# Weight sums of a split-precision mLSTM layer: one sum moved into an accumulating DMA, the heads' work cut into small pieces, four operand buffers

## The chip, the cores and the metric

One core of a Trainium2 chip runs the whole kernel. The metric is the device time of one execution in microseconds (us), taken as the median of several executions; lower is better. Instructions go to TensorE (PE: matmuls, with PEld for its weight loads), VectorE (DVE), ScalarE (ACT), GpSimd (POOL) and SyncE (SP). Here SP does nothing but start DMAs, and POOL, after a few constants, nothing else either.

## The reference

One pre-norm residual layer with an mLSTM token mixer; 256 tokens, model width 4096, 8 heads, query and key width 256, value width 512, all in float32:

```python
hn = rms_norm(x, norm_w)
u = hn @ w_in                                   # 4096 x (4096 qk, 4096 v, 4096 og, 4096 z, 16 gates)
qk = silu(causal_dwconv(qk, conv_w, conv_b))    # 4 taps
# per head, in chunks of 128 tokens with carried state:
#   a = exp(decay) * (q k^T);  num = a v;  hc = num / max(|sum a|, exp(-m))
hn = hc * rsqrt(mean(hc * hc) + EPS) * out_norm_w
y = hn * sigmoid(og) * silu(z)
out = x + y @ w_out                             # 4096 x 4096
```

Nearly all of the arithmetic is the two products with the weight matrices.

## The kernel before

**Products in split precision.** A float32 operand is used as a sum of two parts of a narrower type, `hi` (a rounded copy, made by ACT, L134) and `lo` (the rest, a subtraction on DVE, L135). `matmul3` (L137) issues three matmuls for each product: hi x hi (L139), hi x lo (L140), lo x hi (L141). The activations (`lhs`) are split once; the weights stream through once, in blocks of 128 x 1024 (512 KB), and each block or sum of blocks that is used costs one ACT and one DVE instruction over 1024 columns (`operand`, L143).

**Pairs.** The weights are used in 19 passes, called pairs: two column groups of 512 at a time. For each head there is a pair `oz` (gates of the output), for heads 1 to 7 a pair `qkv`, and at the end four pairs `o0` to `o3` of the output projection. Head 0's query, key and value come from a first stage before them. A pair walks through the 4096 rows in 8 chunks of 512.

**Two kinds of chunk.** Even chunks (`FAST`) use a scheme with seven block products P1 to P7 (in place of eight) on four blocks 11, 12, 21, 22 of weights. It needs four sums of weight blocks, each a DVE addition of 1024 columns: 11+12 (L246, for P5), 22+11 (L252, for P6), 12+22 (L255, for P7), 21+22 (L258, for P4), all updated in place. So a fast chunk has 7 operands, 4 sums and 42 matmuls. Odd (plain) chunks have 4 operands and 48 matmuls. One fast and the plain chunk beside it are called a couple below: 11 operands, 4 sums, 90 matmuls, 8 loads. A pair is four couples.

**Buffers.** Loaded blocks lie in 7 buffers (tag `wraw`, L155); `hi` and `lo` have 3 buffers each (`wpool`, L67). A load starts on SP when the last reader of its buffer is done; ACT can make a `hi` when PE has finished the operand that had the buffer before.

**Combination.** After a pair its seven PSUM banks are put together by four ACT copies (L321) and seven DVE operations (L322 to L328), all written at once behind the pair's last matmul. Then follows the work of the head: convolution (`conv_qk`), decay, scores, values, gates (`gate_y`, L600) and the transposition of the result (`turn`), held in a list `stages` of which one is run at fixed shares (eighths) of the next pair. A head's result is spilled to memory from POOL's queue (L502) and read back in the last `oz` pair (`build_y`), where the left operands of the output projection are built.

**What sets the order.** Each engine runs its own list in order. A scheduler lays these lists out when the program is built, from the order of the code and its own estimates; the lists are fixed then.

Of the kernel before, what the change touches and what calls it, by code (L numbers as in the profile page):

```python
# [61 lines left out]
def mlstm_layer(ctx: ExitStack, tc: tile.TileContext, x, xT, norm_w, w_first, w_in, conv_w, conv_b, gate_b,  # L62
# [125 lines left out]
    lhs = {}  # L188

    def build(c, src):  # L190

        if c in FAST:
            flat = lhs_pool.tile([P, 2 * 7 * HK * P], F32R, name=f"lhs_{c}", tag=f"lhs{c}")
            L = flat.rearrange("p (two s j t) -> p two s j t", two=2, s=7, j=HK)
            a11, a12, a21, a22 = (src[:, j * HK:(j + 1) * HK, t * P:(t + 1) * P]
                                  for t, j in ((0, 0), (0, 1), (1, 0), (1, 1)))
# [9 lines left out]
            names = ("P1", "P2", "P4", "P5", "P6", "P3", "P7")  # L206
            lhs[c] = {s: [[L[:, part, i, j, :] for part in range(2)] for j in range(HK)]
                      for i, s in enumerate(names)}
        else:
            flat = lhs_pool.tile([P, 2 * 3 * CK * P], F32R, name=f"lhs_{c}", tag=f"lhs{c}")  # L210
            L = flat.rearrange("p (two s j t) -> p two s j t", two=2, s=3, j=CK)
            F = big(f"F_{c}", [P, CK, P])
# [5 lines left out]

    def build_x(c):
        src = big(f"xn_{c}", [P, CK, T])  # L220
        nc.sync.dma_start(src, xT[:, c * CK:(c + 1) * CK, :])
        for j in range(CK):
            k = c * CK + j
            nc.vector.scalar_tensor_tensor(src[:, j, :], src[:, j, :], nw[:, k:k + 1], rstdB,
                                           op0=OP.mult, op1=OP.mult)
# [444 lines left out]
```

## Time and profile before

| | us |
|---|---|
| median of 3 runs | 1843.99 (1841.7 to 1845.84) |
| the profiled execution | 1845.81 |
| its span, first to last instruction | 1844.1 |
| PE busy | 1773.2 (96%) |
| DVE busy | 1654.5 (90%) |
| ACT busy | 1135.5 (62%) |
| POOL busy | 12.1 (1%) |
| data moved by DMA | 365.67 MB, mean 198 GB/s |

Busy time is the union of an engine's instructions. Matmuls are pipelined: one is shown with some 390 ns, but in an undisturbed stretch the next one starts 0.23 us after it. So the time from one pair to the next, and the distance between matmul starts, tell more of PE's stalls than its busy share does. "Landing" of a DMA is counted from the issuing instruction's start.

### The profile page before, as it was taken

What the parts mean: (1) busy time and instruction counts of PE and PEld (TensorE: products, weight loads), DVE (VectorE), ACT (ScalarE), POOL (GpSimd) and SP (SyncE); (2) the same over time, 40 slices, a digit from 0 to 9 for tenths busy, and PEclk for the clock granted to TensorE, in tenths of its full rate; (3) what the DMA queues carried; (4) which work ended last, traced back from release to release, by engine and by line L of the source; (5) the groups of instructions that cost most, each with busy time, mean ns of one, the idle gap of its engine ahead of it and who ended that gap; (6) DMA issues with size and microseconds to landing.
All of it is one profiled execution on the core that took longest, in us unless ns stands there. A gap on an engine that the chain in (4) does not pass through costs nothing.

```text
span 1844.1 us, 21723 instructions
## 1 busy us (share of the span) xinstructions
PE 1773.2 (96%) x7804; PEld 1410.7 (77%) x7804; DVE 1654.5 (90%) x1882; ACT 1135.5 (62%) x1303; POOL 12.1 (1%) x29
## 2 busy tenths in 40 slices
PE   9888999999999999999999999999998899999998
PEld 8766787777777878787878787878776668787776
DVE  5799999998999899989998989898989998989887
ACT  6565765665566556656666666566656665565654
POOL 0000000000000000000000000000000000000000
PEclk9899999999999999999999999999999999999999
DMA  9654465556555555565556555655556556766563
GB/s 365 230 189 171 161 220 188 196 174 216 193 183 180 197 192 184 189 200 188 184 198 209 185 187 197 205 183 183 194 194 214 177 189 217 236 210 233 189 206 126
DMA packets 107724, 365.67 MB, mean 198 GB/s; under 512 B 12128, under 2 KB 12512, under 8 KB 107616
## 3 DMA queue, kind: packets, MB, share of 16 engines
q1 hardware_dynamic: 105360, 356.95, 57.9%
q0 software_dynamic: 1968, 6.82, 1.0%
q8 instruction: 61, 1.00, 0.2%
q10 hardware_dynamic: 288, 0.52, 0.1%
q14 instruction: 47, 0.39, 0.1%
HBM read 356.38 MB, written 7.86 MB: 198 GB/s over the span
## 4 chain that ended last, share of the span: by engine, by line
PE 69%; DVE 19%; issue 7%; ACT 3%; DMA 2%; SPq 0%; DVEq 0%; ACTq 0%
PE P_qkv L140 9%; PE P_qkv L141 9%; PE P_qkv L139 9%; PE P_oz L140 9%; PE P_oz L141 8%; PE P_oz L139 8%; PE P_o L140 4%; PE P_o L141 4%; PE P_o L139 4%; DVE wl_oz_P L135 2%; DVE wl_oz L135 2%; DVE lhs L135 1%; DVE w_oz L246 1%; DVE wl_o_P L135 1%; DVE wl_o L135 1%
## 5 line engine op out<-in xcount | busy, mean ns | idle before, releaser
L134 ACT ACTIVATE wh_oz_P<-w_oz 128x1024 fp32r<-128x1024 f32 x224 | 237.6, 1061 | 109.0 <-PE P_oz L141 91.7
L135 DVE TENSOR_TENSOR wl_oz_P<-w_oz,wh_oz_P 128x1024 fp32r<-128x1024 f32 x224 | 270.8, 1220 | 20.2 <-ACT wh_oz_P L134 18.4
L135 DVE TENSOR_TENSOR wl_qkv_P<-w_qkv,wh_qkv_P 128x1024 fp32r<-128x1024 f32 x196 | 237.1, 1221 | 43.4 <-ACT wh_qkv_P L134 40.7
L134 ACT ACTIVATE wh_qkv_P<-w_qkv 128x1024 fp32r<-128x1024 f32 x196 | 208.1, 1062 | 82.5 <-PE P_qkv L141 73.2
L140 PE MATMUL P_oz<-wl_oz,lhs 128*128 128x512 f32 x512 | 205.1, 401 | 11.4 <-DVE wl_oz L135 10.3
L134 ACT ACTIVATE wh_oz<-w_oz 128x1024 fp32r<-128x1024 f32 x128 | 135.5, 1059 | 128.0 <-PE P_oz L141 74.0
L139 PE MATMUL P_oz<-wh_oz,lhs 128*128 128x512 f32 x512 | 190.7, 401 | 18.4 <-ACT wh_oz L134 17.4
L134 ACT ACTIVATE wh_qkv<-w_qkv 128x1024 fp32r<-128x1024 f32 x112 | 118.8, 1061 | 143.1 <-PE P_qkv L141 126.4
L141 PE MATMUL P_oz<-wh_oz,lhs 128*128 128x512 f32 x512 | 201.6, 394 | 0.0
L140 PE MATMUL P_qkv<-wl_qkv,lhs 128*128 128x512 f32 x448 | 178.7, 399 | 4.0 <-DVE wl_qkv L135 4.0
L140 PE MATMUL P_oz<-wl_oz_P,lhs 128*128 128x512 f32 x448 | 179.4, 401 | 1.1 <-DVE wl_oz_P L135 1.1
L139 PE MATMUL P_oz<-wh_oz_P,lhs 128*128 128x512 f32 x448 | 178.6, 403 | 2.0 <-ACT wh_oz_P L134 2.0
L141 PE MATMUL P_oz<-wh_oz_P,lhs 128*128 128x512 f32 x448 | 176.7, 394 | 0.0
L141 PE MATMUL P_qkv<-wh_qkv,lhs 128*128 128x512 f32 x448 | 175.7, 392 | 0.0
L135 DVE TENSOR_TENSOR wl_oz<-w_oz,wh_oz 128x1024 fp32r<-128x1024 f32 x128 | 156.1, 1219 | 21.1 <-ACT wh_oz L134 21.1
L139 PE MATMUL P_qkv<-wh_qkv,lhs 128*128 128x512 f32 x448 | 162.1, 395 | 4.8 <-ACT wh_qkv L134 4.8
L135 DVE TENSOR_TENSOR wl_o_P<-w_o,wh_o_P 128x1024 fp32r<-128x1024 f32 x112 | 135.3, 1222 | 24.6 <-ACT wh_o_P L134 23.1
L135 DVE TENSOR_TENSOR wl_qkv<-w_qkv,wh_qkv 128x1024 fp32r<-128x1024 f32 x112 | 136.6, 1220 | 21.8 <-ACT wh_qkv L134 21.7
L140 PE MATMUL P_qkv<-wl_qkv_P,lhs 128*128 128x512 f32 x392 | 155.2, 396 | 0.0
L134 ACT ACTIVATE wh_o_P<-w_o 128x1024 fp32r<-128x1024 f32 x112 | 118.9, 1061 | 58.9 <-PE P_o L141 56.1
L139 PE MATMUL P_qkv<-wh_qkv_P,lhs 128*128 128x512 f32 x392 | 152.8, 394 | 1.5 <-ACT wh_qkv_P L134 1.5
L141 PE MATMUL P_qkv<-wh_qkv_P,lhs 128*128 128x512 f32 x392 | 153.5, 391 | 0.0
(223 smaller groups left out, 3468.1 us busy)
## 6 DMA issues: line engine op xcount, KB each, us to landing
w_oz<-in_w_in SPq DMA_DIRECT2D x256, 512.0 KB, 4.3
w_qkv<-in_w_in SPq DMA_DIRECT2D x224, 512.0 KB, 4.3
w_o<-in_w_out SPq DMA_DIRECT2D x128, 512.0 KB, 4.4
...
wf<-in_w_first SPq DMA_DIRECT2D x15, 512.0 KB, 6.6
xr<-in_x SPq DMA_DIRECT2D x8, 512.0 KB, 7.4
xn<-in_xT SPq DMA_DIRECT2D x8, 512.0 KB, 4.0
...
```

The source lines that it names most:

```text
L134: nc.scalar.activation(hi, src, AF.Copy)
L135: nc.vector.tensor_sub(lo, src, hi.bitcast(F32))
L139: nc.tensor.matmul(ps, a[0], b[0], start=first, stop=False)
L140: nc.tensor.matmul(ps, a[0], b[1], start=False, stop=False)
L141: nc.tensor.matmul(ps, a[1], b[0], start=False, stop=last)
L246: nc.vector.tensor_add(raw["11"], raw["11"], raw["12"])
```

## The change

- The table `STEPS` takes the place of `ORDER` and the code in `made`: it lists the loads, uses and sums of a fast chunk. Block 12 is loaded once into a buffer of its own, and once more by `fetch`: a DMA from POOL's queue that adds the block to buffer 11 in place, issued when P1's split no longer needs 11. That replaces the DVE addition 11+12. The other three sums stay on DVE: 12+22, (11+12)+22 and 21+(that). A fast chunk then has 7 operands, 3 sums and 5 loads (4 on SP, 1 on POOL).
- At the `gap`s of the table one operand of the plain chunk is used.
- `hi` and `lo` have 4 buffers each (before 3), loaded blocks 6 (before 7).
- The combination of a pair, the work of the heads and the building of left operands are cut into small pieces and put into one list `queue`; after each step of a pair as many pieces are run as it takes to empty the list by four steps before the pair's end. A PSUM bank that is still to be read holds back the first matmul into it (`unread`). The left operands of fast chunks are split in 3 instructions per part in place of 7.
- `rsqrt` has 3 Newton steps (before 4). In the first stage the row squares come one chunk earlier, and the operands are built over four chunks (before three).

```diff
-ORDER = ("P1", "P3", "P2", "P5", "P7", "P6", "P4")
-DSUM = 0
+STEPS = (("load", "11"), ("use", "11", "P1"), ("fetch", "11", "12"), ("gap",),
+         ("load", "22"), ("load", "12"), ("use", "22", "P3"), ("add", "12", "22"), ("gap",),
+         ("use", "11", "P5"), ("add", "11", "22"), ("use", "12", "P7"), ("gap",),
+         ("load", "21"), ("use", "11", "P6"), ("use", "21", "P2"), ("add", "21", "11"), ("gap",),
+         ("use", "21", "P4"))
...
-    wpool = ctx.enter_context(tc.tile_pool(name="wpool", bufs=3))
+    wpool = ctx.enter_context(tc.tile_pool(name="wpool", bufs=4))
...
-        for it in range(4):
+        for it in range(3):
...
-        raw = wpool.tile([P, RAW], F32, name=f"w_{name}", tag="wraw", bufs=7)[:, :n]
+        raw = wpool.tile([P, RAW], F32, name=f"w_{name}", tag="wraw", bufs=6)[:, :n]
...
-    stages = deque()
+    queue = deque()
+    def pump(n=1):
+        for _ in range(n):
+            if queue:
+                queue.popleft()()
...
-            for s0, s1, v in ((0, 2, t0), (2, 3, a22.rearrange("p (s j) t -> p s j t", s=1)), (3, 7, F)):
-                for a in range(s0, s1):
-                    split(L[:, 0, a], L[:, 1, a], v[:, a - s0])
+            def plain():
+                split(rows[:, 0, :CK], rows[:, 1, :CK], src[:, :, :P])
+                split(rows[:, 0, CK:CK + HK], rows[:, 1, CK:CK + HK], a22)
+            def split_sums():
+                split(rows[:, 0, CK + HK:], rows[:, 1, CK + HK:], F.rearrange("p s j t -> p (s j) t"))
...
+        def prepare(todo):
+            for step in todo:
+                where = at + ("11", "12", "22", "21").index(step[-1]) * P * n
+                if step[0] == "load":
+                    raw[step[1]] = load(f"{name}_{c}_{step[1]}", w, where, n)
+                elif step[0] == "fetch":
+                    nc.gpsimd.dma_start(raw[step[1]], source(w, where, n), accum_op=OP.add)
                 else:
-                    nc.vector.tensor_add(raw["22"], raw["22"], raw["11"])
...
+                    nc.vector.tensor_add(raw[step[1]], raw[step[1]], raw[step[2]])
+        def run(before, b, s, after):
+            prepare(before)
+            h = operand(f"{name}_{c}_{s}", raw[b])
+            prepare(after)
             return [(s, [(lhs[c][s][j], b) for j, b in enumerate(by_k(h))])]
...
-        steps = sorted([((i + 0.5) / len(fast), u) for i, u in enumerate(fast)]
-                       + [((i + 1) / len(plain), u) for i, u in enumerate(plain)], key=lambda v: v[0])
+        steps = []
+        for c in FAST:
+            groups = fast_steps(name, w, off, c)
+            for group in groups:
+                steps += group
+                if plain and group is not groups[-1]:
+                    steps.append(plain.pop(0))
...
+        for n, (c, make, cost) in enumerate(steps):
+            while lhs_of.get(c) != of:
+                pump()
             for s, prods in make():
+                if s not in ps:
+                    while s in unread:
+                        pump()
+                    ps[s] = bank(f"{s}_{name}", s)
                 for a, b in prods:
...
-            if done * NCH >= (popped + 1) * total:
-                popped += 1
-                if stages:
-                    stages.popleft()()
+            pump(-(-len(queue) // max(1, len(steps) - 4 - n)))
...
-        tt(A[:, 0], ps["P2"], p1, op=OP.add)
-        tt(B[:, 0], B[:, 0], B[:, 1], op=OP.add)
-        tt(p1, ps["P6"], p1, op=OP.subtract)
-        tt(r7, r7, p1, op=OP.add)
-        tt(B[:, 0], B[:, 0], p1, op=OP.add)
-        tt(B[:, 1], B[:, 1], r7, op=OP.add)
-        tt(A[:, 1], ps["P4"], r7, op=OP.subtract)
-        return A, B
+        return A, B, [read("P2", A[:, 0], ps["P2"], p1, OP.add), read("P6", p1, ps["P6"], p1, OP.subtract),
+                      read("", r7, r7, p1, OP.add), read("P4", A[:, 1], ps["P4"], r7, OP.subtract),
+                      read("", B[:, 0], B[:, 0], B[:, 1], OP.add), read("", B[:, 0], B[:, 0], p1, OP.add),
+                      read("", B[:, 1], B[:, 1], r7, OP.add)]
```

How the instructions stand now, at two places. The first is DVE's list in pair `qkv3`, from the end of one couple into the next. `wl_qkv3_2_P4` is the lo part of operand P4 of chunk 2, `wl_qkv3_3_3` that of plain chunk 3's last block; `w_qkv3_4_12` is the loaded block 12 of chunk 4, and a row that writes and reads `w_` is a sum. Before:

```order
L135 TENSOR_TENSOR wl_qkv3_2_P6_5137<-w_qkv3_2_22_5033,wh_qkv3_2_P6_5136 128x1024
L135 TENSOR_TENSOR wl_qkv3_2_P4_5148<-w_qkv3_2_21_5063,wh_qkv3_2_P4_5147 128x1024
L135 TENSOR_TENSOR wl_qkv3_3_3_5160<-w_qkv3_3_3_5157,wh_qkv3_3_3_5159 128x1024
L135 TENSOR_TENSOR wl_qkv3_4_P1_5178<-w_qkv3_4_11_5175,wh_qkv3_4_P1_5177 128x1024
L135 TENSOR_TENSOR wl_qkv3_4_P3_5190<-w_qkv3_4_22_5187,wh_qkv3_4_P3_5189 128x1024
L246 TENSOR_TENSOR w_qkv3_4_11_5175<-w_qkv3_4_11_5175,w_qkv3_4_12_5229 128x1024
L255 TENSOR_TENSOR w_qkv3_4_12_5229<-w_qkv3_4_12_5229,w_qkv3_4_22_5187 128x1024
L135 TENSOR_TENSOR wl_qkv3_5_0_5202<-w_qkv3_5_0_5199,wh_qkv3_5_0_5201 128x1024
```

And now:

```order
L138 TENSOR_TENSOR wl_qkv3_2_P2_5093<-w_qkv3_2_21_5080,wh_qkv3_2_P2_5092 128x1024
L285 TENSOR_TENSOR w_qkv3_2_21_5080<-w_qkv3_2_21_5080,w_qkv3_2_11_4959 128x1024
L138 TENSOR_TENSOR wl_qkv3_3_3_5106<-w_qkv3_3_3_5103,wh_qkv3_3_3_5105 128x1024
L138 TENSOR_TENSOR wl_qkv3_2_P4_5122<-w_qkv3_2_21_5080,wh_qkv3_2_P4_5121 128x1024
L285 TENSOR_TENSOR w_qkv3_4_12_5164<-w_qkv3_4_12_5164,w_qkv3_4_22_5162 128x1024
L138 TENSOR_TENSOR wl_qkv3_4_P1_5134<-w_qkv3_4_11_5131,wh_qkv3_4_P1_5133 128x1024
L138 TENSOR_TENSOR wl_qkv3_5_0_5147<-w_qkv3_5_0_5144,wh_qkv3_5_0_5146 128x1024
L138 TENSOR_TENSOR wl_qkv3_4_P3_5167<-w_qkv3_4_22_5162,wh_qkv3_4_P3_5166 128x1024
L138 TENSOR_TENSOR wl_qkv3_5_1_5180<-w_qkv3_5_1_5177,wh_qkv3_5_1_5179 128x1024
L138 TENSOR_TENSOR wl_qkv3_4_P5_5196<-w_qkv3_4_11_5131,wh_qkv3_4_P5_5195 128x1024
L285 TENSOR_TENSOR w_qkv3_4_11_5131<-w_qkv3_4_11_5131,w_qkv3_4_22_5162 128x1024
```

The sum 12+22 stands ahead of P1's split, with two splits between it and the sum 21+11 of the chunk before; P5's split comes four places behind P1's. In the first chunk of a pair P1's split stands ahead of the sum.

The second place is SP's list of loads for the couple of chunks 4 and 5 of the same pair. Before:

```order
L156 DMA w_qkv3_4_11_5175<-in_w_in 128x1024
L156 DMA w_qkv3_4_22_5187<-in_w_in 128x1024
L156 DMA w_qkv3_5_0_5199<-in_w_in 128x1024
L156 DMA w_qkv3_4_21_5217<-in_w_in 128x1024
L156 DMA w_qkv3_4_12_5229<-in_w_in 128x1024
L156 DMA w_qkv3_5_1_5242<-in_w_in 128x1024
L156 DMA w_qkv3_5_2_5271<-in_w_in 128x1024
L156 DMA w_qkv3_5_3_5311<-in_w_in 128x1024
```

And now:

```order
L159 DMA w_qkv3_4_11_5131<-in_w_in 128x1024
L159 DMA w_qkv3_5_0_5144<-in_w_in 128x1024
L159 DMA w_qkv3_4_22_5162<-in_w_in 128x1024
L159 DMA w_qkv3_4_12_5164<-in_w_in 128x1024
L159 DMA w_qkv3_5_1_5177<-in_w_in 128x1024
L159 DMA w_qkv3_5_2_5216<-in_w_in 128x1024
L159 DMA w_qkv3_4_21_5234<-in_w_in 128x1024
L159 DMA w_qkv3_5_3_5257<-in_w_in 128x1024
```

Block 12 moves from fifth to fourth place and 21 from fourth to seventh. With six buffers, block 12 takes the buffer that block 11 of the fast chunk before had, so it waits for that chunk's sum 21+11; before, it waited for the split of P6.

## Rows read from the trace of the kernel before

**Rows 1.** The page: busy time, share of the span and instructions of each engine.

```profile
PE 1773.2 (96%) x7804; PEld 1410.7 (77%) x7804; DVE 1654.5 (90%) x1882; ACT 1135.5 (62%) x1303; POOL 12.1 (1%) x29
```

**Rows 2.** Window view, by pair: start:end us, length, busy us (instructions), clock, DMA share, GB/s.

```profile
286.30:376.80 90.50, 88.93 (x392) 70.68 (x391) 84.25 (x93) 57.54 (x66) 0.00 (x0) 1.00 0.55 186
376.80:465.10 88.30, 86.79 (x376) 69.08 (x375) 78.81 (x86) 54.85 (x60) 0.54 (x1) 1.00 0.59 197
1358.30:1461.10 102.80, 91.97 (x388) 70.18 (x386) 98.66 (x132) 66.80 (x94) 0.00 (x0) 0.98 0.57 194
1461.10:1556.50 95.40, 89.78 (x381) 69.46 (x380) 88.02 (x108) 59.19 (x73) 0.00 (x0) 1.00 0.62 204
1556.50:1643.10 86.60, 84.82 (x361) 66.78 (x360) 76.51 (x72) 48.56 (x49) 2.18 (x4) 1.00 0.66 219
```

**Rows 3.** View of line 321 (first of the copies behind a pair): duration, first and last start.

```profile
L321 ACT ACTIVATE p_qkv<-P_qkv x7: 576/579/581, 286.3 to 1358.3; 128x512 f32<-128x512 f32 x7
...
L321 ACT ACTIVATE p_o<-P_o x4: 576/580/581, 1556.5 to 1817.3; 128x512 f32<-128x512 f32 x4
```

**Rows 4.** Timeline of PE, steady stretch: start us, us, instruction.

```profile
446.50 0.39 PE L139 MATMUL P_qkv<-wh_qkv,lhs 128*128 128x512 f32 x1
446.74 0.39 PE L140 MATMUL P_qkv<-wl_qkv,lhs 128*128 128x512 f32 x1
```

**Rows 5.** Chain of waits, four transpositions: start us, us, what.

```profile
420.87 0.44 PE py L492 x4
```

**Rows 6.** Waits of PE: waiting line, releaser, us in total, times, longest us.

```profile
PEld P_oz L139 <- ACT wh_oz L134: 29.0, 37, 3.5
```

**Rows 7.** Timeline of PE loads and DVE, pair qkv2: start us, us, instruction, idle before.

```profile
404.48 0.68 DVE L326 TENSOR_TENSOR B_oz<-B_oz,p_oz 128x512 f32<-128x512 f32 x1
...
406.58 0.19 PEld L139 LDWEIGHTS P_qkv<-wh_qkv,lhs 128*128 128x128 f32 x1 [1.12 <-ACT wh_qkv L134]
...
407.35 0.68 DVE L327 TENSOR_TENSOR B_oz<-B_oz,r_oz 128x512 f32<-128x512 f32 x1
407.48 0.19 PEld L140 LDWEIGHTS P_qkv<-wl_qkv,lhs 128*128 128x128 f32 x1 [0.71 <-DVE wl_qkv L135]
```

**Rows 8.** Groups by line: busy us, mean ns of one, idle us before, releaser.

```profile
L135 DVE TENSOR_TENSOR wl_qkv_P<-w_qkv,wh_qkv_P 128x1024 fp32r<-128x1024 f32 x196 | 237.1, 1221 | 43.4 <-ACT wh_qkv_P L134 40.7
L134 ACT ACTIVATE wh_qkv_P<-w_qkv 128x1024 fp32r<-128x1024 f32 x196 | 208.1, 1062 | 82.5 <-PE P_qkv L141 73.2 <-PE P_oz L141 4.9 <-DVE y L475 0.6
...
L246 DVE TENSOR_TENSOR w_qkv<-w_qkv,w_qkv 128x1024 f32<-128x1024 f32 x28 | 34.1, 1218 | 0.0
...
L135 DVE TENSOR_TENSOR lhs<-F,lhs 128x256 fp32r<-128x256 f32 (+1 forms) x40 | 17.9, 471 | 0.0
...
L325 DVE TENSOR_TENSOR r_oz<-r_oz,p_oz 128x512 f32<-128x512 f32 x8 | 5.5, 686 | 0.0
```

**Rows 9.** DMA view: issues, KB each, median us to landing.

```profile
w_qkv<-in_w_in SPq DMA_DIRECT2D x224, 512.0 KB, 4.3
...
wf<-in_w_first SPq DMA_DIRECT2D x15, 512.0 KB, 6.6
...
spill<-yT POOLq DMA_DIRECT2D x7, 512.0 KB, 3.6
```

**Rows 10.** The page: DMA queues, packets, MB, share of 16 engines.

```profile
q1 hardware_dynamic: 105360, 356.95, 57.9%
```

**Rows 11.** Landing of the seven spills (POOL queue, 512 KB each), 250 to 1330 us.

```profile
DMA to landing us min/median/max: 3.0/3.6/4.2
```

**Rows 12.** Landing of loads of qkv blocks, 500 to 1300 us.

```profile
DMA to landing us min/median/max: 3.3/4.2/6.2
```

**Rows 13.** Window view, first stage and a stretch of pairs.

```profile
0.00:100.00 100.00, 91.49 (x538) 82.35 (x539) 67.76 (x124) 62.57 (x100) 1.70 (x10) 0.95 0.84 298
100.00:200.00 100.00, 88.35 (x377) 66.98 (x376) 95.94 (x139) 62.90 (x88) 0.00 (x0) 0.97 0.49 169
600.00:700.00 100.00, 98.47 (x425) 78.22 (x425) 90.13 (x89) 60.21 (x65) 0.53 (x1) 1.00 0.59 195
```

More of the change, by code (lines that the diff above doesn't have):

```diff
@@ L203, in build @@
-            for s0, s1, v in ((0, 2, t0), (2, 3, a22.rearrange("p (s j) t -> p s j t", s=1)), (3, 7, F)):
-                for a in range(s0, s1):
-                    split(L[:, 0, a], L[:, 1, a], v[:, a - s0])
[L206 to L212, printed above, removed]
+            F = big(f"F_{of}_{c}", [P, 4, HK, P])
@@ L213, in build, with plain @@
+            return [sums, more, plain, split_sums]
+        flat = lhs_pool.tile([P, 2 * 3 * CK * P], F32R, name=f"lhs_{of}_{c}", tag=f"lhs{c}")
+        L = flat.rearrange("p (two s j t) -> p two s j t", two=2, s=3, j=CK)
+        F = big(f"F_{of}_{c}", [P, CK, P])
+        def plain():
             nc.vector.tensor_sub(F, src[:, :, :P], src[:, :, P:])
-            for i, v in enumerate((src[:, :, :P], src[:, :, P:], F)):
-                split(L[:, 0, i], L[:, 1, i], v)
+            split(L[:, 0, 0], L[:, 1, 0], src[:, :, :P])
@@ L216, in build, with rest @@
+        def rest():
+            split(L[:, 0, 1], L[:, 1, 1], src[:, :, P:])
+            split(L[:, 0, 2], L[:, 1, 2], F)
             lhs[c] = {s: [[L[:, part, i, j, :] for part in range(2)] for j in range(CK)]
                       for i, s in enumerate(("T0", "T1", "D"))}
+            lhs_of[c] = of
+        return [plain, rest]
     def build_x(c):
         src = big(f"xn_{c}", [P, CK, T])
[L221 to L225, printed above, removed]
@@ L229, in fast_steps, with lazy, run @@
+    def lazy(make, n):
+        made = []
+        def run(i):
+            if not made:
+                made.extend(make())
+            made[i]()
+        return [lambda i=i: run(i) for i in range(n)]
+    unread = set()
     def fast_steps(name, w, off, c):
@@ new lines, in run @@
+        def run(before, b, s, after):
+            prepare(before)
+            h = operand(f"{name}_{c}_{s}", raw[b])
+            prepare(after)
+            return [(s, [(lhs[c][s][j], b) for j, b in enumerate(by_k(h))])]
+        todo, group, groups = [], [], []
+        for step in STEPS + (("gap",),):
+            if step[0] == "gap":
+                group[-1][-1].extend(todo)
+                groups.append([(c, lambda g=g: run(*g), 1) for g in group])
+                todo, group = [], []
+            elif step[0] == "use":
+                group.append((todo, step[1], step[2], []))
+                todo = []
+            else:
+                todo.append(step)
@@ L270, in plain_steps @@
+        return groups
     def plain_steps(name, w, off, c):
@@ L569, in mlstm_layer @@
     hs, finish = head(0)
[L570 to L579 removed]
+    for c in range(5, NCH):
+        queue.extend(build_x(c))
+    queue.extend([gate_stages[0]] + conv_qk(0, u0) + gate_stages[1:] + hs)
     off = 0
@@ L583, in mlstm_layer, with between @@
     for n, (what, h, _, _) in enumerate(pairs):
-        def between(c, share, n=n):
-            if builds and share * 8 > NCH - len(builds) - 5:
-                f, b = builds.popleft()
-                f(b)
-            if n == len(pairs) - 1 and c is not None and c < HEADS - 1:
-                build_y(c)
-        ps = project_pair(f"{what}{h}", w_in, off, between)
+        def between(c, n=n):
+            if n == len(pairs) - 1 and c < HEADS - 1:
+                queue.extend(build_y(c))
@@ L628, in blocks_of @@
+        queue.extend([lambda residual=residual: (residual(0), residual(1))] + res[2])
+        queue.extend([lambda i=i, t=t, store=store: store(i, t) for i in (0, 1) for t in range(NT)])
+    while queue:
+        pump()
 def blocks_of(w, s1, s2):
```

240 lines of the change are left out of this document (112 added, 128 removed).

## Prediction

> **What bounds the kernel now.** I read the busy shares first [rows 1]. PE shows 96% and DVE 90%, so either could be the bound; busy time alone does not decide it, since matmuls overlap. I therefore took the length of a pair from the copies that follow it. From the first to the last `qkv` copy there are six heads: (1358.3 - 286.3) / 6 = 178.7 us for a `qkv` and an `oz` pair, 89.3 per pair; of the output pairs one takes (1817.3 - 1556.5) / 3 = 86.9 [rows 3]. Against that stands what PE needs: matmul starts lie 0.23 us apart where nothing disturbs [rows 4], so the 360 matmuls of a pair need 82.8. An `oz` pair has 32 further matmuls and a `qkv` pair 16 [rows 2]; transpositions take 0.44 / 4 = 0.11 each [rows 5], those with 512 columns 0.23. With 16 at 0.11, 9 at 0.23 and some 21 at an estimated 0.12, a head's own matmuls take about 6.4 us, 3.2 per pair. So PE's floor is 86.0 in a head's pair and 82.8 in an output pair, and PE stands still for 3.3 and 4.1 us of them.
>
> PE is thus the bound, with small stalls. They have the form of [rows 7]: the combination of the pair before (each operation 0.68) stands between DVE's splits, and a weight load sits 1.12 us for ACT's `hi` and then 0.71 for DVE's `lo`. In total the largest of these waits is 29.0 us [rows 6]. The two places where DVE itself is the bound are the first `oz` pair (DVE 95.94 of 100 us, [rows 13]) and the last `oz` and the first output pair, 102.8 and 95.4 long with DVE at 98.66 and 88.02 [rows 2]. All that can be won: 13 pairs from 195.9 to 1358.3 at 3.3, three at 4.1, (102.8 - 89.3) + (95.4 - 86.9) = 22 at the end, some 15 in the first pair: about 90 us.
>
> **The change part by part.**
>
> *The sum 11+12.* It takes 1.22 on DVE [rows 8], four times per pair: 4.9 us of DVE per pair, 93 in all. DVE is not the bound in most pairs, so this is no gain by itself. What it costs is a new wait. P5's `hi` now waits for a DMA that starts only after P1's `lo`. DVE's list has three splits in between, so DVE waits at P5 when the fetch takes longer than 3 x 1.22 less ACT's 1.06 for P5's `hi` [rows 8]. Behind it stand, in order, P5, the sum 11+22, P7, a plain split, P6, P2 and 21+11: the whole rest of the couple. A second wait comes from six buffers in place of seven: block 12 takes the buffer that 21+11 of the chunk before frees, and the sum 12+22 stands two splits behind that sum and ahead of P1's split. So the two waits lie in one loop of DVE: the sum 12+22 and P1 (2.44), the fetch T, P5's `hi` (1.06), seven operations (8.54), the landing L of block 12. That is 12.0 + T + L per couple, against 90 x 0.23 = 20.7 on PE.
>
> *L.* Loads of 512 KB land in 3.3 at least and 4.2 in the median [rows 12]. Block 12 is issued two splits after any other load, so I take 3.6, near the low end; the ends are 3.3 and 6.2.
>
> *T.* No row shows an accumulating DMA. The nearest rows are the spills, 512 KB from POOL's queue: 3.0, 3.6 and 4.2 [rows 11]. Adding must read the old content as well as the new. The 16 engines spent 57.9% of 1844.1 us on 356.95 MB [rows 10], 1.6 us per 512 KB, so a second stream costs 1.6 when it overlaps the first one's latency. This gives 4.6 from the fastest spill, 5.2 from the median; I take 4.9. Ends: 3.0 (the addition is free) and 8.5 (slowest spill 4.2, then a whole load of 4.3 [rows 9] for the old content).
>
> The Trainium skill (Collectives: The Full Stack, section The bandwidth ceiling: the fold count and why AG ≠ RS ≠ AR) says that an add in the DMA path is slower because it takes two source reads, not because of the addition. By that rule the low end falls away and T would be 5.2; no run here shows it.
>
> *The sum for a pair.* With T = 4.9 and L = 3.6 the loop takes 20.5 per couple, just under PE's 20.7. The first couple of a pair has P1 ahead of the sum, so only the fetch shows: 14 x 1.22 = 17.1 and 4.9 + 1.06 - 4 x 1.22 = 1.1 of waiting, 18.2. Three loops and this give 79.8. DVE's other work in a pair is (84.25 + 78.81) / 2 = 81.5 [rows 2] less 60 x 1.22 = 8.3; DVE waits 3 x 3.4 + 1.1 = 11.3 in the loops, where it can lie. The lists show it inside and outside of the waits; I count half, 4.2. DVE then needs 84.0 per pair, PE 86.0. So PE stays the bound, with 2.0 us to spare. Each us of T costs DVE 4 us per pair: the spare time is gone at T = 5.4, and the 89.3 of before is reached at T = 6.2. In an output pair the other work is 76.51 - 73.2 = 3.3, half of it 1.7: DVE 81.5, PE 82.8.
>
> *Spreading and the fourth buffer.* The combination moves from one block into single pieces between the splits, and ACT and DVE can run one operand (1.4 to 2.8 us of PE) further ahead. A burst of 7 x 0.686 = 4.8 [rows 8] then no longer meets a reserve of two operands. Not all stalls go, as the two DVE waits use the same reserve: I leave 1.0 of 3.3 in a head's pair and 1.5 of 4.1 in an output pair. That is 87.0 and 84.3: 13 x 2.3 = 30 and 3 x 2.6 = 8 us less.
>
> *The places bound by DVE.* Three pairs lose 4.9 each; a fast chunk's left operand takes 0.686 + 0.471 + 1.22 = 2.4 in place of 7 x 0.471 = 3.3 [rows 8], five times in these pairs: 4.6. Together 19; the loops' waits are partly filled, so I count 12.
>
> *At nothing:* the earlier row squares (the first stage moves 298 GB/s at 84% DMA share [rows 13], the bytes are the same), the Newton step (operations on two columns), the end of the kernel, which has the same eleven DVE operations behind the last matmul. If the earlier squares do delay the first loads, it is by one of eight 512 KB transfers at most, 1.6 us. What is late next, once stalls go, is PE itself.
>
> Sum: 30 + 8 + 12 = 50 from the span of 1844.1, so 1794. The profiled execution took 1845.81, 1.7 above its span and 1.8 above the median of the runs; against the median I forecast 1793.
>
> **The rivals.**
>
> *Hidden altogether.* T is 4.2 or less, or more of the head's work lies in the waits; DVE has room, and four buffers take up the bursts. Then pairs come to 86.2 and 83.1 (13 x 3.1 + 3 x 3.8 = 52), and the DVE-bound places give 25 of their 37: 1767. For it: DVE loses 93 us of work. Against: it needs the fetch to land almost like a plain spill.
>
> *Crowded DMA engines.* Each pair moves 4 x 0.5 to 4 x 1.05 MB more on 16.8, so the DMA share of 0.59 [rows 13] rises to 0.66 or 0.74. Loads landed in 6.6 at a share of 0.84 and 4.3 at 0.59 [rows 9, 13]; between these, 0.07 to 0.15 costs 0.6 to 1.4. With 0.9 on T and on L, DVE needs 84.0 + 4 x 0.9 + 3 x 0.9 = 90.3, 1 above before: with the 12 us kept, about 1845. Against: block 12 and the fetch are spaced, and the share counts whole windows.
>
> The Trainium skill (DMA: Bandwidth & Descriptors, section Issuing engines are not separate DMA queues) says that transfers started by SP and by GpSimd share the same 16 engines and interleave. That speaks for this case: POOL's queue brings no bandwidth of its own. No row shows the two kinds beside each other under load.
>
> *The late fetch: slower.* From T = 6.2 on, P5's split holds DVE longer than PE's reserve lasts, in each of 76 fast chunks. At T = 7.0 DVE needs 84.0 + 8.4 = 92.4: 3.1 more than before in 16 head and end pairs, 3 x 3.0 in the output pairs, less 12: 1890. At 8.5 it is 1990. For it: POOL's list is in order and the price of the addition is unknown; spills behind which a fetch stands wait for ACT. Against: plain transfers of this size and queue never took over 4.2.
>
> **How the numbers follow.** The forecast 1793, with its own range of 1770 to 1825 (T from 4.4 to 5.7), has 0.42. Hidden altogether 0.20, crowded engines 0.10, the late fetch 0.28. A measurement of this kernel can tell 0.2%, 3.7 us, from no change. Slower gets the late fetch and little else, 0.27, as its lower edge still falls within the same; same 0.05, from the crowded case; faster 0.68. The range takes all but the edge of the hidden case and the late fetch up to T = 6.9: 1758 to 1885.
>
> **What would show it.** Right: `qkv` copies about 174 us apart per head, output pairs near 84.3; fetches that land 4.6 to 5.3 us after their issue; DVE idle ahead of P5's splits behind ACT, and ACT behind the fetch, in waits of 1 to 2 us that PE does not share; PE busy over 97%. Wrong: fetches of over 6 us with PE waiting for `hi` of P5 in most fast chunks; DVE waiting at the sum 12+22 for block 12 by more than 1.5 us; pairs of 89 us or more; or stalls still at the start of a pair, which would say that buffers and spreading did not reach them.

## The result, and the profile after

The changed kernel takes 1901.63 us (median of 4 runs, 1889.73 to 1902.79) against 1844.76 of the kernel before: 1.0297 times, 95% interval 1.0254 to 1.034. It is slower; 1793 was forecast. The profiled execution, 1889.73 us with a span of 1888.0, is the shortest of the four, so the rows of after hold 44 of the 57 us.

The page of after answers [rows 1, 10]: DVE lost 93 us of work, as expected, and PE has 19 us more busy time for the same matmuls. q0 is POOL's queue, with the 76 fetches, the spills and most writes of the output.

```profile
PE 1792.0 (95%) x7804; PEld 1413.4 (75%) x7804; DVE 1561.0 (83%) x1747; ACT 1078.2 (57%) x1271; POOL 77.0 (4%) x105
...
q1 hardware_dynamic: 105360, 356.95, 54.6%
q0 software_dynamic: 12912, 46.67, 13.4%
```

The first copies behind the pairs [rows 3], now on L362: (1390.3 - 287.4) / 6 = 183.8 us per head, 91.9 per pair against 89.3 before and 87.0 forecast; output pairs (1866.4 - 1587.0) / 3 = 93.1 against 86.9 and 84.3.

```profile
L362 ACT ACTIVATE p_oz<-P_oz x8: 577/580/582, 188.6 to 1482.4; 128x512 f32<-128x512 f32 x8
...
L362 ACT ACTIVATE p_qkv<-P_qkv x7: 577/579/582, 287.4 to 1390.3; 128x512 f32<-128x512 f32 x7
...
L362 ACT ACTIVATE p_o<-P_o x4: 577/581/597, 1587.0 to 1866.4; 128x512 f32<-128x512 f32 x4
```

By pair [rows 2] (start:end, length, busy PE, PEld, DVE, ACT, POOL, granted clock, DMA share, GB/s): all of these pairs have less DVE work, and all but the `oz` pair, 90.0 against 90.5, are longer. DVE is idle for 11 to 18 us of a head's pair, and PE stands still all the same.

```profile
287.40:377.40 90.00, 88.03 (x389) 69.90 (x388) 79.04 (x87) 54.28 (x66) 3.38 (x4) 1.00 0.69 211
377.40:470.10 92.70, 89.59 (x380) 69.33 (x379) 74.58 (x79) 51.69 (x59) 3.95 (x5) 1.00 0.67 210
...
1482.40:1587.00 104.60, 90.49 (x355) 67.04 (x354) 94.06 (x121) 64.50 (x83) 3.40 (x4) 0.95 0.68 218
1587.00:1686.90 99.90, 93.89 (x383) 73.08 (x382) 73.29 (x69) 47.01 (x50) 5.66 (x8) 0.97 0.73 224
```

The DMA view [rows 9, 11] (KB each, median us to landing): fetches land in 5.8 to 6.0 us (5.2 to 8.0 over all 76), loads in 4.5 to 4.8 instead of 4.3 to 4.4, and spills, which share POOL's queue with fetches now, in 8.5 instead of 3.6.

```profile
w_qkv<-in_w_in SPq DMA_DIRECT2D x224, 512.0 KB, 4.7
...
w_oz<-in_w_in POOLq DMA_DIRECT2D x32, 512.0 KB, 5.8
w_qkv<-in_w_in POOLq DMA_DIRECT2D x28, 512.0 KB, 5.9
w_o<-in_w_out POOLq DMA_DIRECT2D x16, 512.0 KB, 6.0
...
spill<-yT POOLq DMA_DIRECT2D x7, 512.0 KB, 8.5
```

The timeline of DVE over one couple in pair `qkv2` (start us, us, instruction, idle before it) shows the loop of the prediction. P1's `lo` ends at 439.67 + 1.22 = 440.89. POOL issues the fetch 0.30 later; ACT can make P5's `hi` at 447.07, so T is 6.18. DVE has three splits for this time and then idles 3.87 us. The sum 21+11 ends at 456.46, the sum 12+22 of the next chunk starts at 460.81, 1.92 of it waiting for block 12: L is 4.35 here, which is long. From P1 to P1: 461.95 - 439.67 = 22.3 us, where PE needs 20.7. Over all couples inside the head pairs, T is 6.2 in the median and 6.5 in the mean, and L 3.2 in the mean (1.9 to 4.7).

```profile
439.67 1.22 DVE L138 TENSOR_TENSOR wl_qkv_P<-w_qkv,wh_qkv_P 128x1024 fp32r<-128x1024 f32 x1
440.81 1.22 DVE L138 TENSOR_TENSOR wl_qkv<-w_qkv,wh_qkv 128x1024 fp32r<-128x1024 f32 x1
441.94 1.22 DVE L138 TENSOR_TENSOR wl_qkv_P<-w_qkv,wh_qkv_P 128x1024 fp32r<-128x1024 f32 x1
443.08 1.22 DVE L138 TENSOR_TENSOR wl_qkv<-w_qkv,wh_qkv 128x1024 fp32r<-128x1024 f32 x1
448.17 1.22 DVE L138 TENSOR_TENSOR wl_qkv_P<-w_qkv,wh_qkv_P 128x1024 fp32r<-128x1024 f32 x1 [3.87 <-ACT wh_qkv_P L137]
...
455.23 1.23 DVE L285 TENSOR_TENSOR w_qkv<-w_qkv,w_qkv 128x1024 f32<-128x1024 f32 x1
...
460.81 1.23 DVE L285 TENSOR_TENSOR w_qkv<-w_qkv,w_qkv 128x1024 f32<-128x1024 f32 x1 [1.92 <-DMA w_qkv<-in_w_in]
461.95 1.22 DVE L138 TENSOR_TENSOR wl_qkv_P<-w_qkv,wh_qkv_P 128x1024 fp32r<-128x1024 f32 x1
```

POOL and ACT in the same stretch:

```profile
441.19 0.84 POOL L283 DMA_DIRECT2D w_qkv<-in_w_in  x1 [19.88 <-DVE wl_qkv_P L138]
...
447.07 2.01 ACT L137 ACTIVATE wh_qkv_P<-w_qkv 128x1024 fp32r<-128x1024 f32 x2 [5.20 <-DMA w_qkv<-in_w_in]
```

The waits (us in total, times, longest) of the `qkv` pairs: ACT for DMAs, DVE for ACT, PE for ACT, and DVE for block 12. `wl_qkv_P` and `wh_qkv_P` stand for all seven operands of a fast chunk; before, DVE waited 40.7 us at these splits [rows 8]. PE seldom waits for P5 itself: its weight loads wait for P5's `hi` in 8 of the 76 chunks, 8.7 us in all, but 37 times and 43.0 us for the `hi` of P6, which comes later in DVE's list.

```profile
ACT wh_qkv_P L137 <- DMA w_qkv<-in_w_in: 132.5, 27, 6.9
...
DVE wl_qkv_P L138 <- ACT wh_qkv_P L137: 97.6, 31, 6.0
...
PEld P_qkv L142 <- ACT wh_qkv_P L137: 24.5, 27, 1.6
...
DVE w_qkv L285 <- DMA w_qkv<-in_w_in: 22.9, 19, 2.3
```

### The profile page after: what moved, and what is told of

It is laid out like the page before. It is cut to its first block, busy times and chain, and to the rows that moved or that the text cites. A ratio compares the mean times of both kernels' runs of the same rounds, so it can differ in the third digit from the quotient of the medians.

```text
span 1888.0 us, 21821 instructions
## 1 busy us (share of the span) xinstructions
PE 1792.0 (95%) x7804; PEld 1413.4 (75%) x7804; DVE 1561.0 (83%) x1747; ACT 1078.2 (57%) x1271; POOL 77.0 (4%) x105
## 5 line engine op out<-in xcount | busy, mean ns | idle before, releaser
L137 ACT ACTIVATE wh_oz_P<-w_oz 128x1024 fp32r<-128x1024 f32 x224 | 228.8, 1053 | 247.3 <-DMA w_oz<-in_w_in 112.6
L137 ACT ACTIVATE wh_qkv_P<-w_qkv 128x1024 fp32r<-128x1024 f32 x196 | 200.4, 1054 | 254.3 <-DMA w_qkv<-in_w_in 132.5
L143 PE MATMUL P_oz<-wl_oz,lhs_x 128*128 128x512 f32 x512 | 205.4, 401 | 5.4 <-DVE wl_oz L138 5.2
L144 PE MATMUL P_oz<-wh_oz,lhs_x 128*128 128x512 f32 x512 | 201.1, 393 | 0.0
L137 ACT ACTIVATE wh_o_P<-w_o 128x1024 fp32r<-128x1024 f32 x112 | 114.2, 1054 | 148.0 <-DMA w_o<-in_w_out 70.9
L142 PE MATMUL P_oz<-wh_oz,lhs_x 128*128 128x512 f32 x512 | 189.6, 397 | 3.9 <-ACT wh_oz L137 3.7
L142 PE MATMUL P_oz<-wh_oz_P,lhs_x 128*128 128x512 f32 x448 | 171.8, 399 | 13.7 <-ACT wh_oz_P L137 13.5
L143 PE MATMUL P_oz<-wl_oz_P,lhs_x 128*128 128x512 f32 x448 | 179.6, 401 | 4.0 <-DVE wl_oz_P L138 4.0
L138 DVE TENSOR_TENSOR wl_o_P<-w_o,wh_o_P 128x1024 fp32r<-128x1024 f32 x112 | 134.2, 1219 | 57.4 <-ACT wh_o_P L137 56.4
L144 PE MATMUL P_oz<-wh_oz_P,lhs_x 128*128 128x512 f32 x448 | 177.0, 395 | 0.0
L143 PE MATMUL P_qkv<-wl_qkv,lhs_x 128*128 128x512 f32 x448 | 176.0, 393 | 0.0
L144 PE MATMUL P_qkv<-wh_qkv,lhs_x 128*128 128x512 f32 x448 | 175.9, 393 | 0.0
L143 PE MATMUL P_qkv<-wl_qkv_P,lhs_x 128*128 128x512 f32 x392 | 160.4, 409 | 7.7 <-DVE wl_qkv_P L138 7.2
L142 PE MATMUL P_qkv<-wh_qkv_P,lhs_x 128*128 128x512 f32 x392 | 154.2, 404 | 13.9 <-ACT wh_qkv_P L137 13.7
L142 PE MATMUL P_qkv<-wh_qkv,lhs_x 128*128 128x512 f32 x448 | 163.0, 394 | 1.0 <-ACT wh_qkv L137 1.0
L144 PE MATMUL P_qkv<-wh_qkv_P,lhs_x 128*128 128x512 f32 x392 | 154.9, 395 | 0.0
```

Source lines behind the costliest of these rows:

```text
L137: nc.scalar.activation(hi, src, AF.Copy)
L138: nc.vector.tensor_sub(lo, src, hi.bitcast(F32))
L142: nc.tensor.matmul(ps, a[0], b[0], start=first, stop=False)
L143: nc.tensor.matmul(ps, a[0], b[1], start=False, stop=False)
L144: nc.tensor.matmul(ps, a[1], b[0], start=False, stop=last)
```

## The experiments

The theory: the fetch comes late in DVE's fixed list (T), a little helped by block 12 (L). Rivals: DMA engines crowded by the extra bytes; the late block 12 alone; the spreading, the new order or the buffers. All times beside the kernel before on the same chip (1844.3 to 1845.4); "per pair" is taken from the copies, as in [rows 3].

| run | median us | ratio to before, 95% | per pair, heads | per output pair |
|---|---|---|---|---|
| changed kernel | 1901.6 | 1.0297 (1.0254-1.034) | 91.9 | 93.1 |
| VectorE's sum, rest of the change kept | 1802.6 | 0.9767 (0.9753-0.9782) | 87.7 | 85.4 |
| fetch that doesn't add | 1803.0 | 0.9761 (0.9745-0.9778) | 87.0 | 88.7 |
| VectorE's sum + extra fetches, untied | 1849.9 | 1.0015 (0.9995-1.0035) | 90.1 | 85.7 |
| VectorE's sum + extra fetches, in place | 1806.5 | 0.979 (0.9776-0.9805) | 87.6 | 85.6 |
| P7 and P2 ahead of P5 | 1823.7 | 0.9878 (0.9863-0.9892) | 89.3 | 84.3 |
| before + fetch alone | 2015.1 | 1.0916 (1.0888-1.0945) | 99.5 | 96.8 |
| fetch in every other fast chunk | 1820.0 | 0.986 (0.9844-0.9877) | 88.4 | 87.3 |
| mixed | 1801.3 | 0.9763 (0.9748-0.9777) | 87.7 | 84.2 |
| VectorE's sum, 3 operand and 7 load buffers | 1834.9 | 0.9943 (0.9926-0.9959) | 89.2 | 86.3 |
| VectorE's sum, old order of the chunk | 1820.5 | 0.9862 (0.9846-0.9879) | 88.7 | 87.9 |
| before + 4 operand and 6 load buffers alone | 1783.2 | 0.9663 (0.9648-0.9677) | 86.4 | 84.2 |

### The fetch taken out

```diff
-STEPS = (..., ("use", "11", "P1"), ("fetch", "11", "12"), ("gap",),
-         ..., ("use", "22", "P3"), ("add", "12", "22"), ("gap",),
+STEPS = (..., ("use", "11", "P1"), ("gap",),
+         ..., ("use", "22", "P3"), ("add", "11", "12"), ("add", "12", "22"), ("gap",),
```

> The fetch is left out and the sum 11+12 is a VectorE operation again (four more of 1.22 us per pair); spreading, four operand buffers and six load buffers stay. Late fetch: the wait of about 6 us per seven-product chunk is gone, VectorE needs about 86 us per pair and TensorE 86, so pairs near 88 and a time of 1785 to 1815. Crowded DMA engines: the second stream is gone too, so the same 1785 to 1815; this run does not tell these two apart. Late block 12 (six load buffers, sum 12+22 early in the list): at least 1860. Spreading or the order of the lists as the cost: at least 1870.

1802.6: the fetch costs 99 us (1901.6 - 1802.6), all of the loss and more; what is left of the change gains 42. Spreading and the order of the chunk are out as the cause of the loss, and so are six load buffers by themselves; DVE's wait for block 12 goes away together with the fetch, so this run alone does not clear block 12 beside a fetch. The page (q0 without fetches; shares of the chain that ended last) shows PE as the main link again:

```profile
q0 software_dynamic: 1968, 6.82, 1.0%
...
PE 61%; issue 19%; DVE 15%; ACT 2%; DMA 2%; SPq 0%; POOL 0%; DVEq 0%; ACTq 0%; POOLq 0%
```

### A fetch that doesn't add

```diff
-nc.gpsimd.dma_start(raw[step[1]], source(w, where, n), accum_op=OP.add)
+nc.gpsimd.dma_start(raw[step[1]], source(w, where, n))
```

> The fetch stays where it is, from the same queue and with the same wait behind it, but it no longer adds: block 12 overwrites block 11, so the sum is left out. Late fetch, its price in the accumulation: it lands in 3.6 to 4.2 us like a spill instead of 5.9, the loop falls from 22.3 to about 20.5 per couple, and the time is 1790 to 1825. Late fetch, its price in the queue and the first packet: it still lands in over 5 us and the time stays above 1870. Late block 12: VectorE still waits for it and the time is at least 1860.

Same bytes fetched from memory, same queue, same wait, no addition: 1803.0. The DMA view (share of 16 engines; landings):

```profile
q0 software_dynamic: 12912, 46.67, 7.8%
...
w_oz<-in_w_in POOLq DMA_DIRECT2D x32, 512.0 KB, 4.4
w_qkv<-in_w_in POOLq DMA_DIRECT2D x28, 512.0 KB, 4.0
w_o<-in_w_out POOLq DMA_DIRECT2D x16, 512.0 KB, 4.6
```

The fetch now lands in 4.0 to 4.6. Landing some 1.5 us earlier, it costs nothing on balance against DVE's sum (1802.6): head pairs are 0.7 shorter, output pairs 3.3 longer. The queue, the first packet and block 12 are all still there (DVE waits 17.8 us for it in the `qkv` pairs, 22.9 in the changed kernel), so by themselves they are not the price. The engines' time per fetch follows from the shares: without fetches q0 took 0.010 x 1800.4 = 18 us; here 0.078 x 1803.7 = 141, so 123 / 76 = 1.6 us; in the changed kernel 0.134 x 1888.0 = 253, so 235 / 76 = 3.1. The addition doubles it. The Trainium skill (Collectives: The Full Stack, section The bandwidth ceiling: the fold count and why AG ≠ RS ≠ AR) says of ReduceScatter that it is slower than a copy because its add takes two source reads, not for the addition itself. The factor between 3.1 and 1.6 agrees with that; no run here shows the second read itself.

### The same traffic, and nobody waits

```diff
+("add", "11", "12"),                       # VectorE makes the sum
-nc.gpsimd.dma_start(raw[step[1]], source(w, where, n), accum_op=OP.add)
+nc.gpsimd.dma_start(spare[:, :n], source(w, where, n), accum_op=OP.add)
```

> As the run with VectorE's sum, and beside it 76 accumulating DMAs of 512 KB from the same queue at the same places, into a block of device memory that nobody reads: the same kind of traffic, more than with the fetch, and no wait for it. Late fetch: within 10 us of the run with VectorE's sum, 1785 to 1820, with loads landing in 4.6 to 5 us. Crowded DMA engines: the loads are late all the same and the time is 1865 or more.

1849.9, in neither place, because the run was badly built: nothing tied the extra DMAs to their chunks, so POOL issued them back to back in the first 650 us. Its windows (four pairs under them, the next pair, eight pairs without):

```profile
206.20:565.20 359.00, 351.06 (x1540) 281.48 (x1539) 327.12 (x353) 220.35 (x251) 36.49 (x45) 1.00 0.89 254
565.20:674.90 109.70, 87.98 (x376) 70.66 (x375) 79.75 (x84) 54.26 (x60) 6.85 (x9) 0.89 0.69 197
674.90:1376.10 701.20, 694.62 (x3062) 561.82 (x3061) 651.95 (x696) 441.19 (x493) 2.13 (x4) 1.00 0.60 195
```

At a DMA share of 0.89 four pairs took 359.0 us, where the same four take 351.2 in the run with VectorE's sum: 2.0 each. The fifth took 109.7 because a spill stood behind the extra DMAs in POOL's queue, ACT's sigmoid waited for the spill's buffer, and PE for ACT:

```profile
ACT sg L650 <- DMA spill<-yT: 21.5, 1, 21.5
PEld P_qkv L142 <- ACT wh_qkv L137: 20.8, 1, 20.8
```

So it was run again, each DMA tied to its chunk:

```diff
+nc.gpsimd.dma_start(spare[:1, :n], last["lo"][:1, :n].bitcast(F32))   # waits for P1's lo
 nc.gpsimd.dma_start(spare[:, :n], source(w, where, n), accum_op=OP.add)
```

> As the earlier run with 76 extra accumulating DMAs, but each is now tied to its place: a row of P1's lo is first written into the scratch block, so the extra DMA starts some 2 us after P1's split, once per seven-product chunk, where the fetch would start. VectorE makes the sum 11+12 itself and nobody waits for the extra traffic. Late fetch: within 10 us of the run with VectorE's sum (1802.6), so 1798 to 1815, pairs of 87 to 88.5. Crowded DMA engines: 1850 or more.

1806.5, 4 us above the run without the traffic, though the DMA share of the pairs is 0.73, more than the 0.67 to 0.69 of the changed kernel. The two pairs below take 88.7 and 86.6, against 88.6 and 86.7 without the traffic; what is lost is lost before them (280.0 against 275.2). Crowding is worth at most some 4 of the 99 us, and nothing in a steady pair. These sums are written to device memory and not on chip; whether that matters was not tried.

```profile
280.00:368.70 88.70, 87.99 (x393) 71.01 (x392) 83.70 (x92) 56.18 (x67) 5.32 (x8) 1.00 0.73 215
368.70:455.30 86.60, 85.68 (x376) 69.42 (x375) 79.69 (x84) 54.17 (x60) 5.96 (x9) 1.00 0.73 225
```

### More work between P1 and P5

```diff
 ("load", "22"), ("load", "12"), ("use", "22", "P3"), ("add", "12", "22"), ("gap",),
-("use", "11", "P5"), ("add", "11", "22"), ("use", "12", "P7"), ("gap",),
-("load", "21"), ("use", "11", "P6"), ("use", "21", "P2"), ("add", "21", "11"), ("gap",),
+("load", "21"), ("use", "12", "P7"), ("use", "21", "P2"), ("gap",),
+("use", "11", "P5"), ("add", "11", "22"), ("use", "11", "P6"), ("add", "21", "11"), ("gap",),
```

> Only the order of a seven-product chunk changes: P7 and P2 go ahead of P5, so that seven VectorE operations (8.5 us) in place of three stand between P1 and P5. The fetch, its bytes and its queue stay. Late fetch: the wait is covered up to a landing of 7 us, TensorE is the bound again, pairs of 86.5 to 88 and 1770 to 1805, less than the run with VectorE's sum. Crowded DMA engines: the same bytes at the same times, 1870 or more. Spreading as the cost: 1870 or more.

1823.7: 78 of the 99 us come back with the fetch and its bytes in place, but it is 19 us above the expected range. Most of these are in the `qkv` pairs (90.9 against 86.7 with VectorE's sum); `oz` and output pairs are as expected (windows of `oz1`, `qkv2`, `o1`):

```profile
277.90:365.70 87.80, 87.54 (x391) 70.54 (x390) 79.42 (x87) 56.27 (x67) 3.38 (x4) 1.00 0.69 219
365.70:456.60 90.90, 88.57 (x378) 70.80 (x377) 75.84 (x80) 54.27 (x59) 3.95 (x5) 0.98 0.69 210
1542.80:1627.30 84.50, 83.61 (x362) 67.41 (x361) 72.46 (x67) 47.27 (x49) 5.66 (x8) 1.00 0.80 250
```

The fetch is covered: ahead of the `hi` of a fast chunk's operands ACT waits for a DMA twice, 2.8 us in all, against 74 times and 132.5 + 112.6 + 70.9 = 316.0 in the changed kernel. In `qkv2`, where the fetch is issued at 383.21, P5's `hi` starts at 394.00 and waits for PE. What is late there is ACT: a table load and two sigmoids of the head before; DVE's product waits for them, ahead of the chunk's sum, and PE's weight load waits 1.76 us. Right behind, the granted clock falls to the lower of its two levels (1.2 of 2.4 GHz), 0.54 in the stretch shown; the same comes in five of the seven `qkv` pairs. Over the whole run the clock is 0.987 against 0.995 with VectorE's sum, by an estimate up to 15 of the 21 us between the two. In the pair traced this is the new order meeting the head's work, not the fetch.

```profile
383.21 0.84 POOL L283 DMA_DIRECT2D w_qkv<-in_w_in  x1 [22.61 <-DVE wl_qkv_P L138]
...
394.00 1.06 ACT L137 ACTIVATE wh_qkv_P<-w_qkv 128x1024 fp32r<-128x1024 f32 x1 [1.28 <-PE P_qkv L144]
...
395.08 1.28 ACT L647 ACT_TABLE_LOAD   x1
...
398.42 1.23 DVE L650 TENSOR_TENSOR B_oz<-B_oz,sg 128x1024 f32<-128x1024 f32 x1 [2.10 <-ACT sg L648]
...
402.00 0.19 PEld L142 LDWEIGHTS P_qkv<-wh_qkv_P,lhs_x 128*128 128x128 f32 x1 [1.76 <-ACT wh_qkv_P L137]
```

```profile
404.00:407.40 3.40, 3.16 (x9) 2.39 (x10) 3.40 (x5) 1.79 (x3) 0.00 (x0) 0.54 0.53 154
```

These fetches land later than the 5.8 to 6.0 of the changed kernel; why was not tried:

```profile
w_oz<-in_w_in POOLq DMA_DIRECT2D x32, 512.0 KB, 7.3
w_qkv<-in_w_in POOLq DMA_DIRECT2D x28, 512.0 KB, 7.6
```

### The fetch alone, and half of the fetches

```diff
 # the kernel before
 elif s == "P5":
-    raw["12"] = load(...); nc.vector.tensor_add(raw["11"], raw["11"], raw["12"])
+    pass
 elif s == "P7":
+    raw["12"] = load(...)
     nc.vector.tensor_add(raw["12"], raw["12"], raw["22"])
...
-if DSUM and s == "P1":
+if s == "P1":
     nc.gpsimd.dma_start(src, source(w, at + 3 * P * n, n), accum_op=OP.add)
```

> The kernel before with one edit: the sum 11+12 by the accumulating DMA, issued behind P1's split; block 12 is loaded at P7. No spreading, three operand buffers, seven load buffers. Late fetch: the list has two splits (2.4 us) between P1 and the sum 22+11 that needs the fetch, so VectorE waits about 6.3 - 2.4 = 3.9 us in each of 76 chunks less the 1.22 of the sum; slower than before by 40 to 110 us, 1885 to 1955. If the fetch only hurts together with four operand buffers or the spread order: 1830 to 1860.

2015.1, 170 us slower, 60 more than the most expected. DVE's waits at the sum that needs the fetch (us, times, longest) are 167.6 together. That this is near the loss proves little, since more than the fetch is in it: block 12, loaded late by this edit, makes DVE wait another 56.4 us at the sum 12+22 (L253; 21.0 + 18.7 + 16.7), a wait that the kernel before does not have, and the granted clock is 0.977 against 0.992. The fetches land in 6.1 to 7.4 (medians), mostly later than the expectation took them. So a late fetch is dear without spreading and a fourth buffer too, but its share of the 170 is not parted.

```profile
DVE w_qkv L250 <- DMA w_qkv<-in_w_in: 81.4, 28, 4.3
DVE w_oz L250 <- DMA w_oz<-in_w_in: 46.9, 27, 3.0
...
DVE w_o L250 <- DMA w_o<-in_w_out: 39.3, 14, 3.8
...
DVE w_qkv L253 <- DMA w_qkv<-in_w_in: 21.0, 22, 1.6
```

```diff
-for step in STEPS + (("gap",),):
+for step in (FETCHED if c in FAST[::2] else STEPS) + (("gap",),):   # STEPS: VectorE's sum
```

> The changed kernel with the fetch in two of the four seven-product chunks of each pair (0 and 4) and VectorE's sum in the others: half the fetches, each as late as before. Late fetch with a threshold, the model of the prediction: a fetched chunk costs VectorE 6.2 + 1.06 - 3.66 - 1.22 = 2.4 us net, two of them 4.8 per pair, part of which TensorE's lead and VectorE's spare time absorb: 1808 to 1830. If each late fetch passes to the time in full: half of the 99 us, 1845 to 1855. Crowded DMA engines, half of the 4 us measured: 1803 to 1807.

1820.0, inside the range of the threshold: half the fetches cost 17 us, the other half 82, though these fetches land later, in 6.5 to 7.0 (medians). That fits a threshold: a late fetch is cheap as long as DVE's spare time and PE's lead last, and dear after. One of the two chunks kept is a pair's first, where by the prediction's list four splits and not three cover the fetch; the run does not part this from the threshold.

### What the rest of the change is worth

```diff
-wpool = ctx.enter_context(tc.tile_pool(name="wpool", bufs=4))
+wpool = ctx.enter_context(tc.tile_pool(name="wpool", bufs=3))
-raw = wpool.tile([P, RAW], F32, ..., tag="wraw", bufs=6)
+raw = wpool.tile([P, RAW], F32, ..., tag="wraw", bufs=7)
```

> The run with VectorE's sum, with three operand buffers and seven load buffers as before: only the spreading of the head's work and the new order of a chunk are left of the change. If the fourth operand buffer carries the gain: 1830 to 1845, pairs of 89. If the spreading carries it: within 8 us of 1802.6. My estimate is in between, nearer to the second: 1805 to 1818.

1834.9: where the fourth buffer carries the gain, and outside my estimate. Spreading and order (with the small items of the change) gain 10, the buffers 32 more. The opposite edit, buffers alone on the kernel before:

```diff
-wpool = ctx.enter_context(tc.tile_pool(name="wpool", bufs=3))
+wpool = ctx.enter_context(tc.tile_pool(name="wpool", bufs=4))
-tag="wraw", bufs=7
+tag="wraw", bufs=6
```

> The kernel before with four operand buffers and six load buffers instead of three and seven, and nothing else: no spreading, no fetch. The earlier runs left 10 us for spreading and order alone and 32 more with the buffers. If the two add up: 1844.6 - 32, 1808 to 1816. If the buffers only help once the head's work is spread: 1830 to 1845. If one load buffer fewer hurts the old order: above 1845.

1783.2, better than every expectation, and the fastest of all kernels here: 62 us less than before by two numbers, which were not tried one by one. Head pairs take 86.2 and 87.0, which is PE's floor of 86.0 in the prediction; PE is busy in all of a window, and the largest wait of PE falls from 29.0 us [rows 6] to 18.5.

```profile
276.10:362.30 86.20, 86.20 (x380) 69.90 (x379) 81.10 (x87) 54.69 (x62) 0.69 (x1) 1.00 0.60 201
362.30:449.30 87.00, 87.00 (x391) 71.21 (x390) 79.71 (x91) 56.86 (x65) 0.54 (x1) 1.00 0.58 197
```

```profile
PEld P_oz L139 <- ACT wh_oz_P L134: 18.5, 19, 2.4
```

With four buffers, then, the spread and reordered kernel (1802.6) is 19 us slower than the old code (1783.2). One run to part the two:

```diff
 STEPS = (("load", "11"), ("use", "11", "P1"), ("gap",),
+         ("load", "22"), ("use", "22", "P3"), ("load", "21"), ("use", "21", "P2"), ("gap",),
+         ("load", "12"), ("add", "11", "12"), ("use", "11", "P5"), ("add", "12", "22"), ("use", "12", "P7"), ("gap",),
+         ("add", "22", "11"), ("use", "22", "P6"), ("add", "21", "22"), ("gap",),
          ("use", "21", "P4"))
```

> The changed kernel without the fetch and with the products of a chunk in the order of before (P1, P3, P2, P5, P7, P6, P4 and its four sums by VectorE); the spreading of the head's work, four operand buffers and six load buffers stay. Against the run of before with four buffers (1783.2) only the spreading and the places of the plain chunks' steps differ, against the run with VectorE's sum (1802.6) only the order of the chunk. If the new order of the chunk cost the 19 us between those two: 1780 to 1790. If the spreading cost them: 1798 to 1808.

1820.5, in neither place: with the old order the spread kernel is slower still, so the new order gains 18 (with the spreading, and with four buffers), and everything else costs 37: spreading, the new places of the plain steps, and the small items (left operands, row squares, Newton step), which the expectation left out. Which of them does it was not tried.

### A mixture

```diff
-for step in STEPS + (("gap",),):
+for step in (STEPS if name[:3] == "qkv" else LATE) + (("gap",),):   # STEPS: VectorE's sum; LATE: P5 later
```

> Each kind of pair takes what was shorter: qkv pairs the sum by VectorE in the changed kernel's order (86.7 us there, 90.9 with P5 later), oz and output pairs the fetch with P7 and P2 ahead of P5 (87.8 against 88.7, and 84.5 against 88.4 in the second output pair). Late fetch: covered fetches cost nothing, so about 6 x 0.9 + 4 = 9 us less than the run with VectorE's sum: 1790 to 1797. Crowded DMA engines: no gain, 1800 to 1815.

1801.3, 1 us below the run with VectorE's sum and not to be told from it (their intervals overlap). `oz` and output pairs gain as expected, but the `qkv` pairs rise from 86.7 to 88.1. Why they rise was not traced. A covered fetch costs nothing on balance here, and brings nothing.

## Why the prediction was wrong

**The failed step is the size of T**, the time from P1's `lo` until P5's `hi` can start. The mechanism was in the prediction: a loop of 12.0 + T + L on DVE, its rival "the late fetch", break-even at T = 6.2. T was taken as 4.9; in the head pairs it is 6.2 in the median and 6.5 in the mean. Its parts: the addition was put at 1.6 and measured at 5.9 - 4.4 = 1.5 in landing and 3.1 - 1.6 = 1.5 in engine time, right. The base was wrong: I took the spills' 3.0 to 3.6 [rows 11], seven transfers in the whole run; a plain transfer of the same size and queue at this place takes 4.0 to 4.6. And 0.4 between P1's `lo`, POOL's issue and ACT's start was not counted. The loads' 4.2 [rows 12] was the nearer row.

With T = 6.2 alone the prediction's sum is 84.0 + 4 x 1.3 = 89.2, the 89.3 of before: this one term takes the gain away. With the fetch that doesn't add, T is 4.8 in the median and head pairs are 87.0, as forecast. That they meet the forecast so closely is luck in part, as its terms for spreading and buffers were wrong (below).

**What the sum still lacks.** L was put at 3.6 and is 3.2 in the mean; the 4.35 of the couple shown is not typical. With the means of the trace the sum gives 3 x (12.0 + 6.5 + 3.2) + 17.1 + (6.5 + 1.06 - 4.88) + 4.2 = 89.1 per head pair, and 91.9 came out. For output pairs, with T = 6.9 and L = 3.9, it gives 68.4 + 17.1 + 3.1 + 1.7 = 90.3, and 93.1 came out. So loop and threshold held, but 2.8 us per pair, most of the loss, are outside of the sum; their cause stays open. In head pairs they go with the late fetch, since the fetch that doesn't add meets the forecast; output pairs take 88.7 even then, against 84.3 forecast. The first loop of a pair is the longest: in `qkv2` the fetches start at 392.30, 419.15, 441.19 and 463.46, 26.9 apart at first and then 22.0 and 22.3. There the combination and the head's work stand in DVE's list too, which the prediction let lie half in the waits.

**Crowded engines** (0.10): at most 4 us, 2.0 per pair even at a share of 0.89. **Hidden altogether** needed T of 4.2 or less; no fetch landed in under 5.2. **The late fetch** (0.28) is what happened, at a price of 57 us over before. Of its signs, fetches near 6 us showed; PE waiting for P5's `hi` in most fast chunks did not, as PE's lead covers P5 and runs out at the operands behind it.

**Spreading and the fourth buffer** were put at 38 us together. That hides two terms: the buffers alone take 62 off and leave head pairs at 86.4, near the floor of 86.0, with the bursts of [rows 7] in place; the spread kernel, with four buffers and the old order of the chunk, gives 37 of it back. I gave both one credit.

**The places bound by DVE** were to lose 12. `oz7`, `o0` and `o1` together took 284.8 before and 296.6 after; with VectorE's sum 1607.5 - 1327.1 = 280.4. The gain there is 4 us, and the fetch's wait outweighs it. With the buffers alone they take 1587.7 - 1313.3 = 274.4, 10 less than before with all of DVE's work in place, so DVE's work was not their only bound. The first pair ends 7.3 us earlier (188.6 against 195.9), but at 185.4 with the buffers alone, and at 193.9 with the rest of the change on three buffers: most of that gain is the buffers' too.
